# Turning the raw gate and up sums with a matrix that also adds the two halves of the rows

## The chip, the cores and the metric

The kernel runs on one core of a Trainium2 chip. The metric is the device time of one execution in microseconds (us); before the change it is 1862.35 us, the median of three runs that lie between 1861.26 and 1864.24. The profiler took one further execution of the same program, and all rows below are from that one.

## The reference, cut to what matters

The program computes two layers of a hybrid encoder trunk over 256 tokens of width 1024. The change touches only the last sublayer, a mixture of eight SwiGLU experts of which each token takes two, so that an expert sees 64 tokens on average:

```python
top_logit, top_e = lax.top_k(logits, TOP_K)          # TOP_K = 2 of N_EXPERTS = 8
def expert_block(args):                              # D_FF_EXPERT = 3584, d = 1024
    xs, e = args
    hdn = jax.nn.silu(xs @ w_gate[e]) * (xs @ w_up[e])
    return hdn @ w_down[e]
y = jnp.zeros((n, d), jnp.float32).at[row_tok].add(yb.astype(jnp.float32) * row_w[:, None])
```

All weights are float32 and are read once from memory; the eight experts hold 352 MB of them.

## The kernel before, in words

**Steps.** The 3584 hidden columns of an expert are cut into seven chunks of 512. One chunk of one expert is a step, so there are 56 steps. `expert_run` writes their order out by hand: two lanes of four experts each. Lane 0 runs its first three steps alone (`LEAD`), then steps of lane 1 and lane 0 alternate, and lane 1 ends with three steps alone. A step is: the gate sums (`gates` into the PSUM tile `ptg`), the up sums (`gates` into `ptu`), and the two halves of the down product of the step before (`down_steps`, `down`, into `ps_ye`). Each step reads six weight pieces of 128x2048 float32 (1 MiB): two of gate, two of up, two of down. `wload` loads one on the queue of SP into a buffer `wr`.

**Two ways to multiply.** How many tokens an expert got is known only on the chip, so `products` holds both ways under `tc.If(many[0])`. An expert with more than 64 tokens (here: a *full* expert) takes `passes`: each weight piece is split by ScalarE (`wh`, L327) and VectorE (`wl = wr - wh`, L333) into two float32r parts, and TensorE makes three products of 512 columns (L1415, L1418, L1419). An expert with at most 64 tokens (a *half* expert) takes `paired`: the weights are used as float32, unsplit, and two products run at once, one on each half of the array's columns (L1425). The first leaves its sum in rows 0 to 63 of the PSUM tile and the second in rows 64 to 127, each over half of the contraction.

**Adding the halves.** For a half expert the two halves of the rows have to be added. ScalarE copies the whole tile to `fe` (L1441, in `folds`), and TensorE multiplies that copy with `fold[e]`, a matrix that picks the lower half, and accumulates it into the upper half of the same PSUM tile (L1442). The fold of the gate sums is issued at the end of the half expert's branch of the up products; the fold of the up sums stands under its own `tc.If(many[2])` (L1652), between the two halves of the down product of the step before. For a full expert that block is jumped over.

**SiLU, product, turn.** Then `hs = silu(ptg) * ptu` (L1657 on ScalarE, L1661 on VectorE) is made with tokens as rows. In the next step, after its gate products, `turned` transposes it in four blocks into `ps_hT` (L1455), copies that as float32 (`hw`, L1459, used by `paired`) and splits it into `hh` and `hl` (L427, used by `passes`). The down products read `hw` or `hh` and `hl`.

**Order around it.** `in_turn` pins the order of the instructions on each engine to the order in which the code is written. `split()` issues the next weight piece, so the splits of a full expert stand among the instructions above on ScalarE and VectorE. PSUM tiles come from three pools: `qbank` with three banks (gate and up sums, gathered rows `ps_gr`), `fbank` with one (`ps_hT`, `ps_gt`, `ps_pT`), `pbank` with four (down sums). At seven places a new expert's rows are gathered (`gather`: `rows_of`, `turn_rows`, `take`, `take_whole`) while the step before it runs.

Of the kernel before, what the change touches and what calls it, by code (L numbers as in the profile page):

```python
# [20 lines left out]
P = 128  # L21
# [144 lines left out]
def tile_encoder(ctx: ExitStack, tc: tile.TileContext, a: dict, out: bass.AP, cw: dict):  # L166
# [1123 lines left out]
    def moe(l, i, xh, xl, xth, xtl):  # L1290
        with weights("r3", NX, ring=raws), tc.tile_pool(name="mo", bufs=1, reuse_waits="tile") as O:
# [58 lines left out]

            slot2 = sm("slot2")
            V.tensor_scalar(slot2, slot, -float(P), None, op0=OP.add)
# [3 lines left out]
            def gather(e, sl, lane, spare):  # L1356
# [19 lines left out]
                def rows_of(n):  # L1376
                    ns = slice(n * 512, n * 512 + 512)
                    pg = qbank("ps_gr")
                    for i, src in enumerate((xth, xtl)):
                        for hf in range(NH):  # L1380
                            keep(T.matmul(pg, pd[:, hf], src[:, hf, ns], start=i + hf == 0, stop=i + hf == NH))
                    rows = O.tile([P, 512], F32, name="rows", tag="fe", bufs=2)
                    keep(A.activation(rows, pg, AF.Copy))
                    at[n] = rows
# [17 lines left out]
            def expert_run(lanes, sl, late=False, summed=None):  # L1402
# [6 lines left out]

                def products(many, ws, h, l, hw, fold=None):  # L1410


                    def passes():
                        for j, (out, k, wh, wl, _, b, z) in enumerate(ws):
                            i = T.matmul(out, h[:, k], wh, start=b, stop=False)  # L1415
                            if j == 0:
                                turn(many, i)
                            T.matmul(out, h[:, k], wl, start=False, stop=False)  # L1418
                            T.matmul(out, l[:, k], wh, start=False, stop=z)  # L1419

                    def paired():
                        for j in range(0, len(ws), 2):
# [4 lines left out]
                        if fold:  # L1427
                            fold()

                    if many is None:  # L1430
                        passes()
                        return
                    with tc.If(many[0]) as c:
                        passes()
                    with c.Else():
                        paired()

                def folds(e, pt):

                    fe = O.tile([P, 512], F32, name="fe", tag="fe", bufs=2)  # L1440
                    in_turn(A.activation(fe, pt, AF.Copy))  # L1441
                    return lambda: T.matmul(pt[:HALF], fold[e], fe, start=False, stop=True, skip_group_check=True)  # L1442

                def gates(gs, pt, ws, many, fo):
# [6 lines left out]
                    products(many, todo, *gs, fo)  # L1451

                def turned(many, hs):
                    pT = fbank("ps_hT").rearrange("p (f t) -> p f t", f=4)
                    turn(many, *[T.transpose(pT[:, f], hs[:, f * P:f * P + P], ident) for f in range(4)])  # L1455
                    hw = None
                    if many is not None:
                        hw = O.tile([P, 4, P], F32, name="hw", bufs=1)
                        turn(many, A.activation(hw, pT, AF.Copy))  # L1459
                    hh = O.tile([P, 4, P], F32R, name="hh", tag="hh", bufs=2)  # L1460
                    hl = O.tile([P, 4, P], F32R, name="hl", tag="hl", bufs=2)
                    turn(many, *evac_split(hh, hl, pT))
                    return hh, hl, hw

                def down(many, c, cols, rows, hs, ye, ws, fo):

                    todo = []
                    for n in cols:
                        for f in rows:
# [3 lines left out]
                            todo.append((ye[n], f, dh[:, f % 2, ns], dl[:, f % 2, ns], w[:, f % 2, ns], b, z))  # L1473
                    products(many, todo, *hs, fo)

# [60 lines left out]
                def folding(e):  # L1536
                    fold[e] = O.tile([P, HALF], F32, name="fold", bufs=2)
                    V.tensor_scalar(fold[e], ident[:, HALF:], few[:, 0, e:e + 1], None, op0=OP.mult)

# [27 lines left out]

                def down_steps(many, e, c, hs, ye, by_cols=False):

                    split()  # L1570
                    parts = turned(many, hs)
                    split()
# [4 lines left out]
                    for j in range(2):  # L1577
                        cols, rows = ((j,), range(4)) if by_cols else (range(2), (2 * j, 2 * j + 1))
                        down(many, c, cols, rows, parts, ye, ws, None)
                        yield  # L1580
# [36 lines left out]
                for e in {e: 0 for e, c in steps}:  # L1617
                    n = steps.index((e, NC - 1))
                    when(n, "T", end, e)
                    when(n, "U", more, e)  # L1620
                    when(n, "S", more, e)
                    if n + 1 < len(steps):
# [10 lines left out]
                for n, (e, c) in enumerate(steps):  # L1633
                    gs, many, _, ye = states[e]
                    if c == 0 and many is not None:
# [4 lines left out]
                    gates(gs, ptg, ws[0], many, None)  # L1640
                    at(n, "G")
                    go(last)
                    at(n, "T")
                    fg = folds(e, ptg) if many is not None else None
                    gates(gs, ptu, ws[1], many, fg)
                    at(n, "U")
                    split()
                    fu = folds(e, ptu) if many is not None else None
                    at(n, "F")
                    go(last)  # L1650
                    if fu:
                        with tc.If(many[2]):  # L1652
# [11 lines left out]
                    prev = many, e, c, hs, ye  # L1664
                last, comb = down_steps(*prev, by_cols=True), states[prev[1]]
                for gen in last, last, comb, last, comb, comb:
                    go(gen)
# [114 lines left out]
```

## Time and profile before

| | |
|---|---|
| median of three runs | 1862.35 us |
| the profiled execution | 1866.12 us, of which the span from first to last instruction is 1864.3 us |
| TensorE busy over the span | 1714.2 us (92%) |
| VectorE, ScalarE, GpSimd busy | 1073.2, 907.8, 256.9 us |
| granted TensorE clock, mean | 0.953 |
| read from memory | 470.26 MB |
| the expert steps | from about 934 to 1844 us of the span |

Busy shares are means over stages with different limits. A matmul's recorded duration is longer than the distance to the next one, because they are pipelined; the cost of a matmul in a stream is therefore read from the distance of two starts. "PE" is TensorE, "PEld" its weight loads, "PEq" its sequencer, ACT ScalarE, DVE VectorE.

### The profile page before, as it was taken

The numbers are of one execution on the slowest core, as the hardware profiler recorded it, in microseconds if no ns is written. First come the engines' busy times: TensorE is split into PE (matmuls) and PEld (weight loads), VectorE is DVE, ScalarE is ACT, GpSimd is POOL, SyncE is SP. The second block draws the span as 40 slices with busy tenths as digits, with TensorE's granted clock in tenths as the row PEclk, the third lists the DMA queues.
The fourth block names the chain that finished last, engine by engine and source line by source line (L and its number), as shares of the span: only waits on it lengthen the run. The fifth ranks groups of instructions, "written<-read, shape, count | busy, mean of one in ns | idle before, by whom it ended". The sixth has DMA issues, their size and how long they took to land. (4 is left out here: it accounts for less than half of the span.)

```text
span 1864.3 us, 30071 instructions
## 1 busy us (share of the span) xinstructions
PE 1714.2 (92%) x11060; PEld 1196.4 (64%) x11060; DVE 1073.2 (58%) x1754; ACT 907.8 (49%) x1651; POOL 256.9 (14%) x248
## 2 busy tenths in 40 slices
PE   5879999899987898999889999998999999999996
PEld 5767869799977677778675554333334655655564
DVE  6888567665657986576574642210214646556476
ACT  4654445455534763345375643321214546455473
POOL 4637300000024545210100000000000000000000
PEclk8988999999998987999899999999999999999998
DMA  5331245355513332265179999999999999989992
GB/s 217 125 108 70 92 159 203 128 211 204 181 59 102 125 105 78 70 241 211 46 265 347 406 393 395 419 420 419 420 421 391 406 398 356 390 335 400 398 369 87
DMA packets 71302, 473.94 MB, mean 254 GB/s; under 512 B 8768, under 2 KB 12224, under 8 KB 15936
## 3 DMA queue, kind: packets, MB, share of 16 engines
q1 hardware_dynamic: 70384, 466.09, 64.5%
q10 hardware_dynamic: 720, 5.24, 0.8%
q8 instruction: 120, 1.97, 0.4%
q14 instruction: 78, 0.64, 0.1%
HBM read 470.26 MB, written 1.05 MB: 253 GB/s over the span
## 5 line engine op out<-in xcount | busy, mean ns | idle before, releaser
L333 DVE TENSOR_TENSOR wl<-wr,wh 128x1024 fp32r<-128x1024 f32 (+4 forms) x530 | 484.9, 965 | 141.2 <-ACT wh L327 140.3
L327 ACT ACTIVATE wh<-wr 128x1024 fp32r<-128x1024 f32 (+1 forms) x564 | 440.4, 845 | 153.6 <-PE ps_gu L1425 61.0
L1425 PE MATMUL ps_gu<-wr,gw 128*64 128x512 f32 x1120 | 266.6, 605 | 11.4 <-DMA wr<-in_moe_wg_dram 10.7
L1425 PEld LDWEIGHTS ps_gu<-wr,gw 128*64 128x64 f32 x1120 | 82.2, 138 | 160.1 <-issue 154.5
L1425 PE MATMUL ps_ye<-wr,hw 128*64 128x512 f32 x560 | 153.5, 608 | 7.4 <-PEq L1652 7.4
L1459 ACT ACTIVATE hw<-ps_hT 128x512 f32<-128x512 f32 x56 | 33.4, 597 | 234.5 <-PE ps_hT L1455 234.5
L338 POOL TENSOR_TENSOR wl<-wr,wh 128x384 fp32r<-128x384 f32 (+6 forms) x68 | 103.7, 1545 | 290.2 <-ACT wh L327 289.9
L427 DVE TENSOR_TENSOR hl<-ps_hT,hh 128x512 fp32r<-128x512 f32 x56 | 38.7, 691 | 179.1 <-ACTq L319 162.6
L1415 PE MATMUL ps_gu<-wh,xg 128*128 128x512 f32 x336 | 134.5, 400 | 2.8 <-ACT gw L1398 2.2
L1418 PE MATMUL ps_gu<-wl,xg 128*128 128x512 f32 x336 | 131.7, 392 | 0.8 <-DVE wl L333 0.8
L1419 PE MATMUL ps_gu<-wh,xg 128*128 128x512 f32 x336 | 132.1, 393 | 0.0
L1689 POOL TENSOR_TENSOR wr<-wr,lp 128x512 f32<-128x512 f32 x1 | 1.5, 1521 | 933.3 <-ACT wr L1688 933.3
L1441 ACT ACTIVATE fe<-ps_gu 128x512 f32<-128x512 f32 x112 | 66.8, 597 | 106.4 <-PE ps_gu L1419 56.0
L1661 DVE TENSOR_TENSOR hs<-hs,ps_gu 128x512 f32<-128x512 f32 x56 | 38.4, 685 | 118.3 <-PEq L1652 58.8
L1277 PE MATMUL ps_gu<-xTl,wh 128*128 128x256 f32 x352 | 99.0, 281 | 0.0
L1278 PE MATMUL ps_gu<-xTh,wl 128*128 128x256 f32 x352 | 98.8, 281 | 0.0
L1276 PE MATMUL ps_gu<-xTh,wh 128*128 128x256 f32 x352 | 98.8, 282 | 0.0
L1425 PEld LDWEIGHTS ps_ye<-wr,hw 128*64 128x64 f32 x560 | 42.2, 137 | 82.3 <-issue 78.8
L1415 PEld LDWEIGHTS ps_gu<-wh,xg 128*128 128x128 f32 x336 | 63.5, 189 | 18.6 <-ACT gw L1398 2.5
L1442 PE MATMUL ps_gu<-fe,fold 128*64 128x512 f32 x140 | 73.1, 603 | 2.4 <-ACT fe L1441 2.1
L1418 PEld LDWEIGHTS ps_gu<-wl,xg 128*128 128x128 f32 x336 | 63.6, 189 | 14.1 <-DVE wl L333 1.1
L1419 PEld LDWEIGHTS ps_gu<-wh,xg 128*128 128x128 f32 x336 | 63.5, 189 | 14.3
(466 smaller groups left out, 3723.3 us busy)
## 6 DMA issues: line engine op xcount, KB each, us to landing
wr<-in_moe_wg_dram SPq DMA_DIRECT2D x112, 1024.0 KB, 8.9
wr<-in_moe_wu_dram SPq DMA_DIRECT2D x112, 1024.0 KB, 9.2
wr<-in_moe_wd_dram SPq DMA_DIRECT2D x112, 1024.0 KB, 10.2
wr<-in_w_in_dram SPq DMA_DIRECT2D x16, 1024.0 KB, 4.9
wr<-in_ffn_wg_dram SPq DMA_DIRECT2D x11, 1024.0 KB, 4.9
wr<-in_ffn_wu_dram SPq DMA_DIRECT2D x11, 1024.0 KB, 4.9
wr<-in_ffn_wd_dram SPq DMA_DIRECT2D x11, 1024.0 KB, 4.9
wr<-in_xk_dram SPq DMA_DIRECT2D x8, 1024.0 KB, 4.8
```

The source lines that it names most:

```text
L327: act_i = A.activation(h[:, s], raw[:, s], AF.Copy)
L333: dve_i = V.tensor_sub(l[:, m], raw[:, m], R_(h[:, m]))
L338: G.tensor_sub(l[:, m], raw[:, m], R_(h[:, m]))
L1276: T.matmul(ps[:, g], wh[:, k, fs], xh[:, k, :], start=k == 0, stop=False)
L1277: T.matmul(ps[:, g], wh[:, k, fs], xl[:, k, :], start=False, stop=False)
L1278: T.matmul(ps[:, g], wl[:, k, fs], xh[:, k, :], start=False, stop=k == KT - 1)
L1415: i = T.matmul(out, h[:, k], wh, start=b, stop=False)
L1418: T.matmul(out, h[:, k], wl, start=False, stop=False)
L1419: T.matmul(out, l[:, k], wh, start=False, stop=z)
L1425: T.matmul(out[f * HALF:f * HALF + HALF], hw[:, k, :HALF], w, start=ws[j][5], stop=ws[j + 1][6], skip_group_check=True)
L1441: in_turn(A.activation(fe, pt, AF.Copy))
L1442: return lambda: T.matmul(pt[:HALF], fold[e], fe, start=False, stop=True, skip_group_check=True)
```

## The change

The raw sums of the gate and of the up product are both copied to `fe` (`taken`), for every expert. `turned` then multiplies blocks of `fe` with `fold[e]`, now 128x128: the identity and, for a half expert, a second identity that adds the lower half of the rows; for a full expert it is the identity alone. One such product turns a block and adds its halves. There are eight of them, four into `pTs[0]` (gate) and four into `pTs[1]` (up). SiLU and the product are made on the turned tiles and write `hw` directly; the copy to `hw` goes away, and so do both folds and the block under `tc.If(many[2])`. In the last step `turned` stands between the two down halves of the step before it.

```diff
-                def folds(e, pt):
-
+                def taken(pt):
                     fe = O.tile([P, 512], F32, name="fe", tag="fe", bufs=2)
-                    in_turn(A.activation(fe, pt, AF.Copy))
-                    return lambda: T.matmul(pt[:HALF], fold[e], fe, start=False, stop=True, skip_group_check=True)
+                    in_turn(A.activation(fe, pt, AF.Copy)) if sl is slot else A.activation(fe, pt, AF.Copy)
+                    return fe
...
-                def turned(many, hs):
-                    pT = fbank("ps_hT").rearrange("p (f t) -> p f t", f=4)
-                    turn(many, *[T.transpose(pT[:, f], hs[:, f * P:f * P + P], ident) for f in range(4)])
-                    hw = None
-                    if many is not None:
-                        hw = O.tile([P, 4, P], F32, name="hw", bufs=1)
-                        turn(many, A.activation(hw, pT, AF.Copy))
+                def turned(many, e, fes):
+
+                    pTs = [new("ps_hT").rearrange("p (f t) -> p f t", f=4) for new in (fbank, qbank)]
+                    for pT, fe in zip(pTs, fes):
+                        turn(many, *[T.matmul(pT[:, f], fe[:, f * P:f * P + P], fold[e], start=True, stop=True) for f in range(4)])
+                    hs = O.tile([P, 4, P], F32, name="hs", tag="hs", bufs=HSB)
+                    turn(many, A.activation(hs, pTs[0], AF.Silu))
+                    hw = O.tile([P, 4, P], F32, name="hw", bufs=1)
+                    turn(many, V.tensor_mul(hw, hs, pTs[1]))
...
-                    turn(many, *evac_split(hh, hl, pT))
+                    turn(many, *evac_split(hh, hl, hw))
...
-                    fold[e] = O.tile([P, HALF], F32, name="fold", bufs=2)
-                    V.tensor_scalar(fold[e], ident[:, HALF:], few[:, 0, e:e + 1], None, op0=OP.mult)
+                    if sl is not slot:
+                        fold[e] = ident
+                        return
+                    fold[e] = O.tile([P, P], F32, name="fold", bufs=2)
+                    lo, hi = slice(0, HALF), slice(HALF, P)
+                    V.scalar_tensor_tensor(fold[e][:, lo], ident[:, hi], few[:, 0, e:e + 1], ident[:, lo], op0=OP.mult, op1=OP.add)
+                    V.tensor_scalar(fold[e][:, hi], ident[:, hi], few[:, 1, e:e + 1], None, op0=OP.mult)
...
-                    fg = folds(e, ptg) if many is not None else None
-                    gates(gs, ptu, ws[1], many, fg)
+                    fes = [taken(ptg)]
+                    gates(gs, ptu, ws[1], many)
                     at(n, "U")
                     split()
-                    fu = folds(e, ptu) if many is not None else None
+                    fes.append(taken(ptu))
                     at(n, "F")
                     go(last)
-                    if fu:
-                        with tc.If(many[2]):
-                            in_turn(fu())
+                    prev = many, e, c, fes, ye
+                    if n == len(steps) - 1:
+                        final = down_steps(*prev, by_cols=True)
+                        go(final)
                     at(n, "D")
                     go(last)
-                    hs = O.tile([P, 512], F32, name="hs", tag="hs", bufs=HSB)
-                    turn(many, A.activation(hs, ptg, AF.Silu))
                     split()
                     at(n, "S")
                     split()
-                    turn(many, V.tensor_mul(hs, hs, ptu))
```

The same on the engines, in the order of the built program. On PE, between the gate products of a step (L1425 and before) and its up products (L1431 or L1433 and after), the four transposes stood:

```order
L1425 MATMUL ps_gu<-wr,gw_10245 64x512 x8
L1433 UNCONDITIONAL_BRANCH
L1455 MATMUL ps_hT<-consts,hs 128x128 x4
L319 UNCONDITIONAL_BRANCH x3
L1433 COMPARE_AND_BRANCH
```

and now the eight products stand there:

```order
L1425 MATMUL ps_gu<-wr,gw_10240 64x512 x8
L1431 UNCONDITIONAL_BRANCH
L1454 MATMUL ps_hT<-fold,fe 128x128 x8
L319 UNCONDITIONAL_BRANCH
L1431 COMPARE_AND_BRANCH
```

The place is the same; what is multiplied there is no longer the finished `hs`, but the two raw copies. Also on PE, between the two halves of the down product (`ps_ye`), stood the block of the second fold:

```order
L1425 MATMUL ps_ye<-wr,hw 64x512 x4
L1433 UNCONDITIONAL_BRANCH
L319 UNCONDITIONAL_BRANCH x3
L1652 COMPARE_AND_BRANCH
L1442 MATMUL ps_gu<-fe,fold 64x512
L1652 UNCONDITIONAL_BRANCH x2
L1433 COMPARE_AND_BRANCH
```

and now one half follows the other:

```order
L1425 MATMUL ps_ye<-wr,hw 64x512 x4
L1431 UNCONDITIONAL_BRANCH
L1431 COMPARE_AND_BRANCH
```

The branch L1652 is gone for all experts, the fold with it. On DVE, around the place in a step where `hl` is made, only the subtraction stood between two weight splits (L333), and the product `hs` (L1661) followed later:

```order
L333 TENSOR_TENSOR wl<-wr,wh 128x1024 x2
L319 UNCONDITIONAL_BRANCH x2
L427 TENSOR_TENSOR hl<-ps_hT,hh 128x512
L319 COMPARE_AND_BRANCH
L333 TENSOR_TENSOR wl<-wr,wh 128x1024 x2
```

and now the product stands there too:

```order
L333 TENSOR_TENSOR wl<-wr,wh 128x1024 x2
L319 UNCONDITIONAL_BRANCH x2
L1458 TENSOR_TENSOR hw<-hs,ps_hT 128x512
L427 TENSOR_TENSOR hl<-hw,hh 128x512
L319 COMPARE_AND_BRANCH
```

The product moved from the end of its own step into the chain that ends in `hw`, `hh` and `hl` of the next one. Besides, `rows` of a gather uses the buffer of `hs` in place of one of the two of `fe`, and `slot2` reuses the buffer of `sel`; a gather now meets a step in which `pTs[1]` and the up sums have the same PSUM bank.

## Rows read from the trace of the kernel before

**Rows 1.** The page: memory traffic in 40 equal slices of the span.

```profile
GB/s 217 125 108 70 92 159 203 128 211 204 181 59 102 125 105 78 70 241 211 46 265 347 406 393 395 419 420 419 420 421 391 406 398 356 390 335 400 398 369 87
```

**Rows 2.** Stretches: length, busy time by engine (x count), clock, DMA share, GB/s.

```profile
1055.38:1086.76 31.38, 30.89 (x134) 17.74 (x133) 16.75 (x17) 17.01 (x22) 0.00 (x0) 1.00 1.01 402
...
1152.15:1164.90 12.75, 12.75 (x57) 4.68 (x57) 1.38 (x2) 2.77 (x5) 0.00 (x0) 1.00 1.01 421
...
1248.82:1266.15 17.33, 14.67 (x58) 5.12 (x57) 1.38 (x2) 2.77 (x5) 0.00 (x0) 0.90 1.02 422
...
1805.55:1824.00 18.45, 18.13 (x81) 14.57 (x80) 18.19 (x20) 14.37 (x17) 0.00 (x0) 1.00 0.91 359
```

**Rows 3.** Timeline of PE over two steps: start, duration, instruction, count, [idle before].

```profile
1055.97 3.65 PE L1425 MATMUL ps_gu<-wr,gw 128*64 128x512 f32 x16
1059.65 1.07 PE L1442 MATMUL ps_gu<-fe,fold 128*64 128x512 f32 x2
1060.65 0.50 PE L1415 MATMUL ps_ye<-wh,hh 128*128 128x512 f32 x1
...
1063.64 1.07 PE L1442 MATMUL ps_gu<-fe,fold 128*64 128x512 f32 x2
...
1067.55 0.39 PE L1415 MATMUL ps_gu<-wh,xg 128*128 128x512 f32 x1
...
1073.04 0.60 PE L1455 MATMUL ps_hT<-consts,hs 128*128 128x128 f32 x4
...
1079.05 1.94 PE L1425 MATMUL ps_ye<-wr,hw 128*64 128x512 f32 x8
1081.46 1.94 PE L1425 MATMUL ps_ye<-wr,hw 128*64 128x512 f32 x8 [0.47 <-PEq L1652]
1083.23 3.60 PE L1425 MATMUL ps_gu<-wr,gw 128*64 128x512 f32 x16
1086.76 0.66 PE L1455 MATMUL ps_hT<-consts,hs 128*128 128x128 f32 x4
```

**Rows 4.** Line L1652: all that PE's sequencer did for its block.

```profile
L1652 PEldq EVENT_SEMAPHORE  x20: 51/51/51, 964.8 to 1833.6; - x20
```

**Rows 5.** Groups by line: count, busy us, mean ns, idle before.

```profile
L1442 PE MATMUL ps_gu<-fe,fold 128*64 128x512 f32 x140 | 73.1, 603 | 2.4 <-ACT fe L1441 2.1
L1455 PE MATMUL ps_hT<-consts,hs 128*128 128x128 f32 x224 | 35.4, 280 | 1.2 <-DVE hs L1661 1.2
L1459 ACT ACTIVATE hw<-ps_hT 128x512 f32<-128x512 f32 x56 | 33.4, 597 | 234.5 <-PE ps_hT L1455 234.5
L1661 DVE TENSOR_TENSOR hs<-hs,ps_gu 128x512 f32<-128x512 f32 x56 | 38.4, 685 | 118.3 <-PEq L1652 58.8 <-PE ps_gu L1442 58.2
```

**Rows 6.** Timeline of weight loads and matmuls outside the experts.

```profile
856.02 0.19 PEld L404 LDWEIGHTS ps_f<-xTl,wh 128*128 128x128 f32 x1
856.14 0.19 PEld L405 LDWEIGHTS ps_f<-xTh,wl 128*128 128x128 f32 x1
...
858.22 1.46 PE L1201 MATMUL ps_xs<-wr,qx 128*128 128x256 f32 x6
```

**Rows 7.** Timeline of PE at the start of the expert steps.

```profile
947.22 0.49 PE L1415 MATMUL ps_gu<-wh,xg 128*128 128x512 f32 x1 [0.32 <-PEq L1652]
...
951.76 0.50 PE L1418 MATMUL ps_gu<-wl,xg 128*128 128x512 f32 x1 [0.76 <-DVE wl L333]
...
955.77 0.66 PE L1455 MATMUL ps_hT<-consts,hs 128*128 128x128 f32 x4 [1.22 <-DVE hs L1661]
```

**Rows 8.** Timeline of PE at the end of the expert steps.

```profile
1838.56 0.50 PE L1415 MATMUL ps_ye<-wh,hh 128*128 128x512 f32 x1 [1.24 <-ACT hh L427]
```

**Rows 9.** Timeline of PE in a step in which rows are gathered.

```profile
1643.76 0.63 PE L1381 MATMUL ps_gr<-xtokl,pd 128*128 128x512 f32 x2
...
1649.72 0.66 PE L1389 MATMUL ps_gt<-consts,rows 128*128 128x128 f32 x4 [1.12 <-ACT gw L1398]
```

**Rows 10.** Timeline of VectorE in a full expert's step.

```profile
1068.89 2.36 DVE L333 TENSOR_TENSOR wl<-wr,wh 128x1024 fp32r<-128x1024 f32 x2
```

More of the change, by code (lines that the diff above doesn't have):

```diff
@@ L1349, in counting @@
                 V.tensor_scalar(upper, iotas, HALF - 0.5, -float(HALF), op0=OP.is_gt, op1=OP.mult)
-            slot2 = sm("slot2")
+            slot2 = sel
             V.tensor_scalar(slot2, slot, -float(P), None, op0=OP.add)
@@ L1381, in rows_of @@
                             keep(T.matmul(pg, pd[:, hf], src[:, hf, ns], start=i + hf == 0, stop=i + hf == NH))
-                    rows = O.tile([P, 512], F32, name="rows", tag="fe", bufs=2)
+                    rows = O.tile([P, 512], F32, name="rows", tag="fe" if spare is pbank else "hs", bufs=2 if spare is pbank else HSB)
                     keep(A.activation(rows, pg, AF.Copy))
@@ L1408, in expert_run, with products @@
                 turn = lambda many, *ins: [in_turn(i) for i in ins if many is not None]
-                def products(many, ws, h, l, hw, fold=None):
+                def products(many, ws, h, l, hw):
                     def passes():
@@ L1426, in paired @@
                                          skip_group_check=True)
-                        if fold:
-                            fold()
                     if many is None:
@@ L1436, in products, with gates @@
                         paired()
-                def folds(e, pt):
+                def taken(pt):
                     fe = O.tile([P, 512], F32, name="fe", tag="fe", bufs=2)
-                    in_turn(A.activation(fe, pt, AF.Copy))
-                    return lambda: T.matmul(pt[:HALF], fold[e], fe, start=False, stop=True, skip_group_check=True)
-                def gates(gs, pt, ws, many, fo):
+                    in_turn(A.activation(fe, pt, AF.Copy)) if sl is slot else A.activation(fe, pt, AF.Copy)
+                    return fe
+                def gates(gs, pt, ws, many):
                     todo = []
@@ L1450, in gates, with down @@
                             todo.append((pt, k, wh[:, k4], wl[:, k4], w[:, k4], k == 0, k == KT - 1))
-                    products(many, todo, *gs, fo)
-                def turned(many, hs):
-                    pT = fbank("ps_hT").rearrange("p (f t) -> p f t", f=4)
-                    turn(many, *[T.transpose(pT[:, f], hs[:, f * P:f * P + P], ident) for f in range(4)])
-                    hw = None
-                    if many is not None:
-                        hw = O.tile([P, 4, P], F32, name="hw", bufs=1)
-                        turn(many, A.activation(hw, pT, AF.Copy))
+                    products(many, todo, *gs)
+                def turned(many, e, fes):
[6 more added lines that the diff above has]
+                    turn(many, V.tensor_mul(hw, hs, pTs[1]))
                     hh = O.tile([P, 4, P], F32R, name="hh", tag="hh", bufs=2)
                     hl = O.tile([P, 4, P], F32R, name="hl", tag="hl", bufs=2)
-                    turn(many, *evac_split(hh, hl, pT))
+                    turn(many, *evac_split(hh, hl, hw))
                     return hh, hl, hw
-                def down(many, c, cols, rows, hs, ye, ws, fo):
+                def down(many, c, cols, rows, hs, ye, ws):
                     todo = []
@@ L1473, in down @@
                             todo.append((ye[n], f, dh[:, f % 2, ns], dl[:, f % 2, ns], w[:, f % 2, ns], b, z))
-                    products(many, todo, *hs, fo)
+                    products(many, todo, *hs)
                 def combine(e, many, ye, first):
@@ L1566, in split, with down_steps @@
                             made[key] = wload("moe_w" + w, i * NE + e, j * 4, 4, c * 512, 512, held, cond)
-                def down_steps(many, e, c, hs, ye, by_cols=False):
+                def down_steps(many, e, c, fes, ye, by_cols=False):
                     split()
-                    parts = turned(many, hs)
+                    parts = turned(many, e, fes)
                     split()
@@ L1578, in down_steps @@
                         cols, rows = ((j,), range(4)) if by_cols else (range(2), (2 * j, 2 * j + 1))
-                        down(many, c, cols, rows, parts, ye, ws, None)
+                        down(many, c, cols, rows, parts, ye, ws)
                         yield
@@ L1620, in expert_run @@
                     when(n, "U", more, e)
-                    when(n, "S", more, e)
+                    when(n, "F", more, e)
                     if n + 1 < len(steps):
@@ L1634, in expert_run @@
                     gs, many, _, ye = states[e]
-                    if c == 0 and many is not None:
+                    if c == 0:
                         folding(e)
@@ L1639, in expert_run @@
                     last = down_steps(*prev) if prev else None
-                    gates(gs, ptg, ws[0], many, None)
+                    gates(gs, ptg, ws[0], many)
                     at(n, "G")
@@ L1660, in expert_run @@
                     split()
-                    turn(many, V.tensor_mul(hs, hs, ptu))
                     at(n, "M")
                     split()
-                    prev = many, e, c, hs, ye
-                last, comb = down_steps(*prev, by_cols=True), states[prev[1]]
-                for gen in last, last, comb, last, comb, comb:
+                last, comb = final, states[prev[1]]
+                for gen in last, comb, last, comb, comb:
                     go(gen)
```

## The prediction

> **What bounds the kernel now.** Only the expert steps change, so I read these alone, first by memory traffic. In the slices of the page from the 21st on [rows 1] traffic is 390 to 420 GB/s; in a block of six slices it stands at 419 to 421, elsewhere a little lower. The stretches say why [rows 2]. Where both lanes hold half experts, traffic is 421 GB/s with a DMA share of 1.01. A step there brings six pieces of 1 MiB (6.29 MB), which is 14.9 us at that rate, while TensorE needs 12.75 us when it still has pieces in hand and stretches to 17.33 us when it waits. That block, some 270 us long, is bound by memory: what TensorE saves in it is worth nothing. Where a half and a full expert alternate, a pair of steps takes 31.38 us at 402 GB/s and TensorE is busy for 30.89 of them; memory alone would need 2 x 14.9 = 29.9 us. That stretch is bound by TensorE, with only 1.5 us per pair between the two bounds. Where full experts run alone (three steps at each end) a step takes 18.45 us, TensorE is busy for 18.13 and VectorE for 18.19.
>
> The number of steps of each kind follows from the code and from one row: 140 records of the fold [rows 5] are 35 steps with two folds of two records (a float32 product is made in two passes, each a record). So 35 of 56 steps belong to half experts and 21 to full ones, three experts. The order of the products on PE shows which: the first of lane 0 and the last two of lane 1. Of their 21 steps 3 run alone at the start and 3 at the end; 4 and 11 alternate with half steps. So there are 15 pairs that TensorE bounds, and 6 lone full steps. The sum goes over these alone.
>
> **The turn.** Four transposes become eight float32 products of 128 columns, 16 passes in place of 4. Four transposes take 0.60 us with the last one's tail; a single one has a mean of 0.28 [rows 5], so they follow each other at (0.60 - 0.28) / 3 = 0.107 us [rows 3]. No float32 product with 128 weight columns and 128 moving columns stands in the trace. Bounds: from below the transpose's 0.107. Six passes of 256 columns take 1.46 us, less a tail of 0.38 that is 0.216 each [rows 6]: two cycles per column, so 128 columns stream in 0.108 too. What could be slower is the weight load. Loads of 128x128 follow each other at 0.12 us where the products are short [rows 6], and each one lasts 0.19. From above I take that 0.19. The nearest row is the stream of loads, and I use 0.115, between it and the transposes. The turn then costs 16 x 0.115 - 4 x 0.107 = +1.41 us per step. A page's rule on the load stands here for comparison. The Trainium skill (TensorE: Matmul & The Clock Gate, LDWEIGHTS) prices a weight load by its columns over 1.2 GHz, 107 ns for 128; by it the turn would cost 16 x 0.107 - 0.43 = +1.28 us, and the trace's 0.12 us is a little worse.
>
> **The folds (half steps).** The two folds take 1060.65 - 1059.65 = 1.00 us each [rows 3]. Ahead of the first PE waits for the copy: the up products take 3.68 us where the same sixteen passes take 3.53 in the gate products, 0.15. The half of the down product between the folds takes 1063.64 - 1060.65 = 2.99 us, where twelve passes in one run take 5.49 / 2 = 2.75; with no switch between the halves I give back 0.2 for both. Together -2.35 us. With the turn a half step changes by -0.94.
>
> **The skipped block (full steps).** For a full expert the block L1652 is jumped over, and that is not free. Eight passes that start at 1079.05 should hand over after 8 x 0.215 = 1.72 us, at 1080.77; the next start is at 1081.46 [rows 3], 0.69 us later, and PE's sequencer is named. The block leaves a semaphore event on 20 of the 21 full steps [rows 4]. With down products of a full expert the loss is smaller, near 0.47 us (0.32 idle [rows 7] and a slow first pass, estimated at 0.15). Without the block two such halves follow each other with about 0.05. So -0.64 with the turn +1.41 is +0.77 us for a full step in a pair, and -0.45 + 1.41 = +0.96 for a lone one.
>
> **Pairs.** -0.94 + 0.77 = -0.17, for 15 pairs -2.6 us. A pair of 31.2 us stays above memory's 29.9, so memory does not cut it off.
>
> **Start.** In the first two steps SiLU and the product stand ahead of the splits of the next weights, and the turn waits for them: idle times of 0.32, 0.76 and 1.22 us [rows 7], 2.3 in all, and with the slow passes behind them (0.3 each, estimated) some 3.2 us. After the change both come later and the splits are made sooner; TensorE needs the copies alone. VectorE has little in hand there, so I count 2.4 of the 3.2. Two turns +2.8, one skip -0.45: together -0.1 us.
>
> **End.** Two turns of lone full steps +2.8; two skips -0.9. The last turn now takes 1.84 us, its own 0.60 and 1.24 of waiting for the copies, which nothing covers [rows 8]; after the change it stands ahead of a down half of 2.75 us, which covers the chain, and costs 1.84 + 0.1. Together +2.0 us.
>
> **Gathers.** Four of the seven gathers lie in stretches that TensorE bounds. There the second transposition of rows waits for the chain of evictions on ScalarE, not for PE: 5.3 us from the end of `ps_gr` to `ps_gt` [rows 9], with a fold lying in that wait. So the fold's 1.0 us, or the skip's 0.6, is not gained there. Besides the up sums have the bank of `pTs[1]` and must wait for VectorE's product; `ps_gr` covers most of it. I take +1.0 for two half steps and +0.6 for two full ones, +3.2 us.
>
> **What costs nothing.** ScalarE loses a copy of 0.60 us per step, and VectorE keeps its count [rows 5]; in the pairs they are busy for 17 of 31.4 us [rows 2]. The chain from the turn to `hh` grows from two copies to SiLU, product and copy, 0.6 + 0.69 + 0.6 = 1.9 us. The up products, 3.5 us at least, lie over it. VectorE's product stands right behind a weight split of two pieces, 2.36 us, which before is done 1.8 us ahead of the turn (1071.25 against 1073.04) [rows 10, 3]. If that cover went, the down product would wait; that is a rival below. The new matrix is two small instructions per expert on VectorE, ahead of its steps. No DMA is added or moved.
>
> **Sum.** -2.6 - 0.1 + 2.0 + 3.2 = +2.5 us. The profiled execution's 1866.12 us would become 1868.6; it lay 3.8 us above the median of the runs, so against 1862.35 I get about 1864.9. I count the uncertain terms (0.2 for the switch between halves, 0.8 kept back at the start) half towards the gain and forecast **1864 us**, no change that a measurement can tell: for this kernel 0.2%, 3.7 us, is about what can be told from none. Its own range is 1859 to 1868.
>
> **Rivals.**
> (a) *Faster.* The pitch is 0.107, the wait at the start goes entirely, and the gathers keep their gain: the turn then costs 1.28, 0.13 less at each of the 34 turns in TensorE-bound steps (-4.4), the start -0.8, the gathers -3.2. That is -5.9 us against the sum, about **1857**. For it: transposes do run at 0.107, and PE is nowhere idle for ScalarE once folds are gone. Against: 0.12 in the stream of loads, and the wait at `ps_gt` is not PE's.
> (b) *Slower by the weight loads.* If a load of float32 weights is not hidden behind a stream as short as itself, the pitch goes towards 0.19: 34 x 16 x 0.075 = +41 us at the end of that, 1905; halfway, at 0.145, +16 us and **1880**. It decides from 0.12 on, where it adds 2.7 us. Against: loads already follow each other at 0.12 with a product under way.
> (c) *Slower by the chain.* If VectorE's product comes a whole weight split later (2.36 us), the chain lasts 4.5 us against 3.5 of cover in the 15 half steps of the pairs: +15 us, **1879**. It decides once the product is more than 1.4 us late. Against: VectorE is busy for half of that stretch, and before the change it waits for the turn rather than the turn for it.
> (d) *The skip is worth less.* If the stall at L1652 is the drain between two products of different kind, which stays, only the branch instruction itself is saved. From rows the gain would then be only the idle time that names the sequencer's wait event, 0.05 us [rows 4], in place of 0.64 and 0.45: 15 x 0.59 + 3 x 0.4 = +10 us, **1874**. Against: 0.47 us of the gap are put down to the sequencer. The rule of a page would be close to it: the Trainium skill (Advanced Engine Details and Errata, Control Flow Timing) gives 108 ns for a compare-and-branch and 51 ns for a branch, by which the skip would be worth 0.16 us, the time about 1872. The rows do not bear it out, since the gap is four times that.
>
> **Chances.** Forecast 0.45, (a) 0.25, (b) 0.13, (c) 0.09, (d) 0.08. So faster by over 0.2% 0.25, within 0.2% 0.45, slower 0.30. The range that leaves out the far half of (b) and the tails of (a) and (c) is 1854 to 1879.
>
> **What would show it.** In the profile after: 16 passes of the turn at 0.11 to 0.12 us from start to start, about 1.9 us between gate and up products; pairs of about 31.2 us; no gap between two down halves of a full step (now 0.69); the first turn some 2 us earlier than at 955.77; the half-expert block unchanged at about 420 GB/s; two lone full steps at the end about 1 us longer each; a wait of about 1 us more ahead of `ps_gt` in a gather. The prediction is wrong if the turn's pitch is above 0.13, if the down products wait for `hh` or `hw`, or if a pair falls to memory's 29.9 us.

## The result, and the profile after

The changed kernel takes 1887.38 us (median of four runs, 1884.91 to 1889.74) against 1862.15: a ratio of 1.0134, with an interval of 1.0114 to 1.0154. That is 25 us slower. The forecast was 1864 and its range 1854 to 1879, so the prediction was wrong. The profiled execution has a span of 1887.8 us, 23.5 more than before.

First the work itself. The timeline of PE in the changed kernel, over a half and a full step, answers to [rows 3]:

```profile
1054.00 2.05 PE L1454 MATMUL ps_hT<-fold,fe 128*128 128x128 f32 x16
1055.98 3.65 PE L1425 MATMUL ps_gu<-wr,gw 128*64 128x512 f32 x16
1059.57 0.50 PE L1415 MATMUL ps_ye<-wh,hh 128*128 128x512 f32 x1
...
1070.88 1.95 PE L1454 MATMUL ps_hT<-fold,fe 128*128 128x128 f32 x16
...
1078.22 3.65 PE L1425 MATMUL ps_ye<-wr,hw 128*64 128x512 f32 x16
1081.71 3.60 PE L1425 MATMUL ps_gu<-wr,gw 128*64 128x512 f32 x16
```

The turn takes 1.98 us in the half step (1055.98 - 1054.00), and in the full step that follows the sixteen passes of the down product (the half expert's, from the step before) run through in 3.49 us with no gap (1081.71 - 1078.22). The windows of the changed kernel for such a pair, a step of the memory-bound block and a lone full step answer to [rows 2] (length, busy time by engine, clock, DMA share, GB/s):

```profile
1054.00:1085.24 31.24, 31.24 (x154) 20.38 (x153) 16.74 (x17) 16.12 (x20) 0.00 (x0) 1.00 0.99 406
1155.18:1167.61 12.43, 12.43 (x66) 5.22 (x64) 1.38 (x2) 2.42 (x4) 0.00 (x0) 1.00 1.01 422
1825.67:1844.92 19.25, 19.25 (x94) 16.06 (x93) 18.27 (x19) 13.80 (x16) 0.00 (x0) 1.00 0.88 339
```

A pair is 31.24 us where it was 31.38. So the ordinary steps do what was forecast, and the loss must lie in steps that are not ordinary. Setting the start of every turn on PE against the same turn of before gives the place (each length is the distance of two starts in the two timelines; the sums of four and two steps are added up):

| stretch of the expert steps | before, us | after, us | difference | forecast |
|---|---|---|---|---|
| start, up to the second turn | 43.21 | 39.50 | -3.71 | -1.4 |
| ordinary pairs | 408.81 | 406.80 | -2.01 | -2.4 |
| four gathering steps in TensorE-bound stretches | 80.57 | 100.60 | **+20.03** | +4.4 |
| two steps in which a half expert ends ahead of a full step | 37.75 | 41.79 | **+4.04** | with the pairs |
| memory-bound block | 288.11 | 288.99 | +0.88 | 0 |
| end, the last four turns and the products behind them | 55.86 | 59.97 | **+4.11** | +2.0 |

With the 0.24 us by which the stage begins later they make 23.6 us, the 23.5 of the span to the rounding. The forecast column puts each term of the prediction where its steps lie: of the two turns counted in the start (+1.41 each) the second falls in the first gathering step. The four gathering steps are most of the loss. The worst of them is 26.04 us long in place of 18.62. PE in that step of the changed kernel:

```profile
1560.21 1.95 PE L1454 MATMUL ps_hT<-fold,fe 128*128 128x128 f32 x16
1565.16 1.22 PE L1381 MATMUL ps_gr<-xtokh,pd 128*128 128x512 f32 x2 [3.01 <-DVE pd L1361]
...
1567.46 0.63 PE L1418 MATMUL ps_gu<-wl,xg 128*128 128x512 f32 x1
1567.89 0.63 PE L1419 MATMUL ps_gu<-wh,xg 128*128 128x512 f32 x1
```

PE waits 3.01 us for `pd`, the one-hot matrix that picks the rows to be gathered. Then nine passes follow each other at 0.43 us in place of 0.23. Why `pd` is late stands in the timeline of VectorE at the same place:

```profile
1553.29 2.36 DVE L333 TENSOR_TENSOR wl<-wr,wh 128x1024 fp32r<-128x1024 f32 x2 [1.47 <-ACT wh L327]
1562.19 0.28 DVE L1541 SCALAR_TENSOR_TENSOR fold<-consts,few 128x64 f32<-128x64 f32 x1 [6.55 <-PE ps_hT L1454]
1562.40 0.25 DVE L1542 TENSOR_SCALAR fold<-consts,few 128x64 f32<-128x64 f32 x1
1562.56 2.35 DVE L333 TENSOR_TENSOR wl<-wr,wh 128x1024 fp32r<-128x1024 f32 x2
1564.83 0.48 DVE L1361 TENSOR_SCALAR pd<-consts,slot 128x128 fp32r<-128x128 f32 x2
1565.45 0.69 DVE L1458 TENSOR_TENSOR hw<-hs,ps_hT 128x512 f32<-128x512 f32 x1
```

VectorE stands for 6.55 us before the small instruction that makes the fold matrix of the *next* expert, and waits for PE's turn (L1454). The matrix has two buffers. The turn that runs here is the last one that reads the matrix of the lane's old expert, and the new matrix goes into that buffer. Behind the blocked instruction stand a pair of weight splits, then `pd`, then the product. In the code the matrix is made one step later than `pd`; since `in_turn` does not pin it, the built order could put it ahead of `pd` on VectorE, as it did before the change too. The view of waits (total, times, longest) of the changed kernel shows that the blocked instruction stands at every gather but the first:

```profile
DVE fold L1541 <- PE ps_hT L1454: 64.2, 6, 12.0
```

The same instruction waited in the kernel before as well, 25.3 us in five places (L1442 are the folds, the readers of that time), and PE had no wait for `pd` in the expert steps:

```profile
DVE fold L1538 <- PE ps_gu L1442: 14.9, 3, 5.1
...
DVE fold L1538 <- PEq L1652: 10.4, 2, 5.2
```

In two other gathering steps the same blocked queue shows twice, ahead of the gathered rows and ahead of the up sums. The PE timeline of one:

```profile
1120.13 0.73 PE L1381 MATMUL ps_gr<-xtokh,pd 128*128 128x512 f32 x2 [0.98 <-DVE pd L1361]
1123.39 5.35 PE L1425 MATMUL ps_gu<-wr,gw 128*64 128x512 f32 x16 [2.06 <-DVE hw L1458]
```

The second wait is for the product, because the up sums of this step have the PSUM bank of the turned up sums. The last two places: where a half expert ends, and the last step.

```profile
1546.89 0.58 PE L1488 MATMUL ps_pT<-gate,pg 128*128 128x1 f32 x4 [1.94 <-DVE pg L1484]
...
1862.13 0.50 PE L1415 MATMUL ps_ye<-wh,hh 128*128 128x512 f32 x1 [1.51 <-ACT hh L427]
```

### The profile page after: what moved, and what is told of

Its sections match the earlier page's. It is cut to its first block, busy times and chain, and to the rows that moved or that the text cites. A ratio compares the mean times of both kernels' runs of the same rounds, so it can differ in the third digit from the quotient of the medians.

```text
span 1887.8 us, 30968 instructions
## 1 busy us (share of the span) xinstructions
PE 1726.9 (91%) x11592; PEld 1258.0 (67%) x11592; DVE 1076.0 (57%) x1762; ACT 887.2 (47%) x1595; POOL 257.0 (14%) x248
## 5 line engine op out<-in xcount | busy, mean ns | idle before, releaser
L333 DVE TENSOR_TENSOR wl<-wr,wh 128x1024 fp32r<-128x1024 f32 (+4 forms) x530 | 483.9, 965 | 183.4 <-ACT wh L327 182.5
L1425 PE MATMUL ps_gu<-wr,gw 128*64 128x512 f32 x1120 | 259.8, 603 | 13.2 <-DMA wr<-in_moe_wg_dram 9.0
L1425 PEld LDWEIGHTS ps_gu<-wr,gw 128*64 128x64 f32 x1120 | 78.4, 138 | 164.2 <-issue 145.6
L1458 DVE TENSOR_TENSOR hw<-hs,ps_hT 128x512 f32<-128x512 f32 x56 | 38.5, 687 | 196.8 <-PE ps_hT L1454 190.7
L1456 ACT ACTIVATE hs<-ps_hT 128x512 f32<-128x512 f32 x56 | 33.4, 597 | 243.4 <-PE ps_hT L1454 243.4
L1425 PE MATMUL ps_ye<-wr,hw 128*64 128x512 f32 x560 | 131.4, 606 | 2.7 <-DMA wr<-in_moe_wd_dram 2.3
L1454 PEld LDWEIGHTS ps_hT<-fold,fe 128*128 128x128 f32 x896 | 106.2, 191 | 27.3 <-issue 13.8
L1454 PE MATMUL ps_hT<-fold,fe 128*128 128x128 f32 x896 | 112.3, 278 | 0.0
L1425 PEld LDWEIGHTS ps_ye<-wr,hw 128*64 128x64 f32 x560 | 37.3, 137 | 78.5 <-issue 64.0
```

Source lines behind the costliest of these rows:

```text
L333: dve_i = V.tensor_sub(l[:, m], raw[:, m], R_(h[:, m]))
L1454: turn(many, *[T.matmul(pT[:, f], fe[:, f * P:f * P + P], fold[e], start=True, stop=True) for f in range(4)])
```

## The experiments

The first four were made against the changed kernel, each undoing one suspect. All times stand beside the kernel before on the same chip.

**e1: make the fold matrix later.**

```diff
-                    if c == 0:
-                        folding(e)
                     ptg, ptu = qbank("ps_gu"), qbank("ps_gu")
...
+                    if c == 0:
+                        folding(e)
                     at(n, "D")
```

and the two instructions in `folding` are wrapped in `in_turn`.

> The changed kernel (1887.4 us) with the two instructions that make the fold matrix of a new expert moved on VectorE from the start of the expert's first step to its second half, and pinned there. Theory 1 (VectorE is blocked: the new matrix needs the buffer that the turn of the expert before still reads, so the one-hot matrix of the gathered rows, a pair of weight splits and the product queue up behind it): the waits of 3.01, 0.98 and 0.98 us ahead of the gathered rows and two of the three waits for the product's PSUM bank (2.06 each) go, with the slow passes after the longest: 8 to 12 us, about 1877. Theory 2 (the gathers lose their time only because the turned up sums and the next up sums share a bank): PE waits in the same places for the product instead, under 2 us, about 1886.

Measured: 1869.99 us against 1861.10, 1.0045 (1.0028 to 1.0061). That is 17.4 us less than the changed kernel's median (16.6 by the two ratios), more than theory 1 expected, which counted slow passes behind one wait only. In the changed kernel the up products behind the two waits of 2.06 us are slow too (5.35 us in place of 3.65, at a granted clock of 0.68 and 0.67). The three gathering steps fall by 4.9, 5.8 and 3.9 us; the first gather, which no fold matrix blocks, stays at 21.6. VectorE and PE in the worst step of before, now with this edit:

```profile
1552.47 0.48 DVE L1361 TENSOR_SCALAR pd<-consts,slot 128x128 fp32r<-128x128 f32 x2
1556.37 0.69 DVE L1458 TENSOR_TENSOR hw<-hs,ps_hT 128x512 f32<-128x512 f32 x1 [3.42 <-PE ps_hT L1454]
```

```profile
1554.31 1.95 PE L1454 MATMUL ps_hT<-fold,fe 128*128 128x128 f32 x16
1556.02 0.71 PE L1381 MATMUL ps_gr<-xtokh,pd 128*128 128x512 f32 x2
```

`pd` is ready 1.4 us before the turn begins, the rows follow the turn without a wait, and the up sums of these steps no longer wait for the product either, although the banks are as they were. Theory 1 holds. The edit both moves and pins the two instructions; which of the two is needed was not separated.

**e2: another bank for the first gathered rows.**

```diff
-                    pg = qbank("ps_gr")
+                    pg = (fbank if spare is fbank and n == 0 else qbank)("ps_gr")
```

> The changed kernel with the first gathered rows put into the bank of the turned gate sums, so that the up sums of a gathering step get a bank of their own. Theory 1 (VectorE's blocked queue is the larger part): the waits of 1.32, 2.06 and 2.06 us for the product go, but the rows now wait some 0.6 us for SiLU and the later rows for the same late chain: 2 to 4 us, about 1884. Theory 2 (the shared bank is the whole loss of the gathers): 10 us or more, about 1876.

Measured: 1881.17 us, 1.0104 (1.0084 to 1.0124), 6.2 less than the changed kernel. That lies between the two theories. The first gather falls by 1.4 us, two others by 2.4 each. The wait for `pd` stays in all three steps that have a blocked matrix, 1.07 us in two and 3.10 us in the third. One of them:

```profile
1116.48 0.70 PE L1381 MATMUL ps_gr<-xtokh,pd 128*128 128x512 f32 x2 [1.07 <-DVE pd L1361]
```

The shared bank is a part of the loss; only in the first gather is it all that goes beyond the turn itself (+1.45 us is left there, for a turn of +1.35). With the fold matrix out of the way (e5 against e1, by step) the bank is worth 1.5 us in the first gather, 0.1 in two others and 1.1 in the last.

**e3: a free buffer for the last product.**

```diff
-                    hw = O.tile([P, 4, P], F32, name="hw", bufs=1)
+                    hw = O.tile([P, 4, P], F32, name="hw", tag="fe" if final else "hw", bufs=2 if final else 1)
```

> The changed kernel with the last step's product written into a free buffer (one of fe) and not into the single buffer hw, which the second down half of the step before still reads. If the wait is for that buffer, the product follows SiLU by itself and PE's wait of 1.51 us ahead of the last down products goes: 1.5 to 2 us less, about 1885.6, and SiLU to product falls from 3.1 us to about 0.1. If the chain itself is too long for the cover of one down half, the wait stays above 1 us.

Measured: 1885.05 us, 1.0124 (1.0104 to 1.0145); the last step falls by 2.0 us. VectorE and then ScalarE at the end of the changed kernel, and VectorE of e3:

```profile
1860.73 0.69 DVE L1458 TENSOR_TENSOR hw<-hs,ps_hT 128x512 f32<-128x512 f32 x1 [3.67 <-PE ps_ye L1419]
...
1857.03 0.60 ACT L1456 ACTIVATE hs<-ps_hT 128x512 f32<-128x512 f32 x1 [1.41 <-PE ps_hT L1454]
```

```profile
1855.05 0.69 DVE L1458 TENSOR_TENSOR hw<-hs,ps_hT 128x512 f32<-128x512 f32 x1 [0.87 <-PE ps_hT L1454]
```

In the changed kernel the product waits for PE's down products (`ps_ye`), 3.1 us beyond the end of SiLU: `hw` has one buffer, and the down half that was meant to cover the chain may itself read it. In e3 it starts 0.3 us after SiLU's end at 1854.75, and PE has no wait there.

**e4: the compares of an ended expert ahead of the product.**

```diff
-                    when(n, "T", end, e)
+                    when(n, "G", end, e)
```

> The changed kernel with the compares of a finished expert's weights (pg) issued on VectorE ahead of the turn's product, and not behind it. If the two waits of 1.94 us ahead of ps_pT come from the longer chain (SiLU, product) that now stands ahead of these compares, both go: 3 to 4 us less, about 1884. If they come from the weight splits ahead of them, they stay and the time stays within 1 us of 1887.4.

Measured: 1879.70 us, 1.0089 (1.0066 to 1.0113), 7.7 less. Both waits are gone; the compares `pg` now come 14 us ahead of their reader:

```profile
1529.46 0.48 DVE L1484 TENSOR_SCALAR pg<-cols,slot 128x128 f32<-128x128 f32 x2
...
1543.56 0.61 PE L1488 MATMUL ps_pT<-gate,pg 128*128 128x1 f32 x4
```

The two steps fall from 20.9 to 17.35 us, 3.5 each and not the 1.94 of the wait, and to 1.5 below the kernel before. The rest is the clock, below.

**e5: all four edits.**

> The changed kernel with all four edits of the first runs: fold matrix made later, first gathered rows in the other bank, the last product in a free buffer, pg ahead of the product. By the steps in which each of them gained (17.4 for the first, 1.4 that the second adds in the first gather, 2.0 for the third, 5.5 that the fourth adds to the first): about 1861, as before the change. If the edits stand in each other's way (pg and the gathers share VectorE), 1866 or more.

Measured: 1860.57 us, 0.9997 (0.9986 to 1.0009). The edits add up; the time is that of the kernel before, to between -2.6 and +1.7 us. So the four account for the loss of the changed kernel. What is left of the change is worth nothing that can be told; the prediction's sum of +2.5 us lies a little above that interval. By stretch e5 keeps gains and losses of its own: against the kernel before the gathers stand at +2.7 us and the end at +1.8, the start at -2.8, the ordinary pairs at -2.0 and the two steps of e4 at -3.0.

**e6: transposes in place of products,** on top of e5. The halves are not added here, and no fold matrix is made.

```diff
-                        turn(many, *[T.matmul(pT[:, f], fe[:, f * P:f * P + P], fold[e], start=True, stop=True) for f in range(4)])
+                        turn(many, *[T.transpose(pT[:, f], fe[:, f * P:f * P + P], ident) for f in range(4)])
```

> As e5, with eight plain transposes in place of the eight float32 products of the turn. It leaves out the adding of the halves of half experts, so it only measures what the products cost. Theory 1 (a product costs two passes of 0.106 us, a transpose one): a turn is 0.85 us shorter; in the pairs of half and full steps the cycle falls from 31.24 to some 29.6 to 29.9 us, where memory binds, and the time falls by 20 to 28 us against e5, to about 1837. Theory 2 (the turn's price is its start and the switch to full width, not the passes): under 8 us.

Measured: 1830.70 us, 0.9850 (0.9833 to 0.9868), 29.9 below e5, a little more than theory 1 gave. The group of the turn and the window of one pair:

```profile
L1454 PE MATMUL ps_hT<-consts,fe 128*128 128x128 f32 x448 | 59.8, 276 | 0.0
```

```profile
1050.40:1079.70 29.30, 29.30 (x138) 18.39 (x137) 16.77 (x17) 16.15 (x21) 0.00 (x0) 1.00 1.01 420
```

448 records against 896 in the changed kernel: one pass for a transpose, two for a product. TensorE is busy for the whole 29.3 us and memory is at the 420 GB/s of the block: both bounds meet here.

**e7: the halves added behind the transposes.**

```diff
+                    up = O.tile([P, 4, HALF], F32, name="up", bufs=1)
+                    for pT, to in zip(pTs, (hs[:, :, :HALF], up)):
+                        turn(many, A.activation(to, pT[:, :, HALF:], AF.Copy, scale=few[:, 0, e:e + 1]))
+                    for pT, to in zip(pTs, (hs[:, :, :HALF], up)):
+                        turn(many, V.tensor_add(pT[:, :, :HALF], pT[:, :, :HALF], to))
                     turn(many, A.activation(hs, pTs[0], AF.Silu))
```

> As e6, with the halves added behind the turn: ScalarE copies the upper 64 columns of both turned tiles, scaled by 1 for a half expert and 0 for a full one, and VectorE adds them to the lower 64 columns, before SiLU. Four instructions of 256 columns more in the chain, some 1.6 us. If the up products (3.5 us and more) still cover the chain, the time is that of e6 within 3 us and beats both kernels; if not, PE waits for hw or hh in each of the 30 steps of the pairs, up to 1 us each, and it ends near 1855.

Measured: 1848.18 us, 0.9939 (0.9916 to 0.9961). It beats both kernels and leaves nothing out, but 17.5 us of e6 are lost. In most pairs the time is that of e6 (15.78 and 13.50 us for the two halves of a pair in both); by step, 7.0 us stand in the first two steps, 4.6 in the last two, and most of the rest at gathers and just behind them. In a lone full step VectorE had no room before either [rows 2]. PE of e7 in three such places:

```profile
960.19 0.50 PE L1415 MATMUL ps_ye<-wh,hh 128*128 128x512 f32 x1 [1.18 <-ACT hh L427]
976.46 1.22 PE L1381 MATMUL ps_gr<-xtokh,pd 128*128 128x512 f32 x2 [3.77 <-ACT hs L1462]
...
1668.46 0.49 PE L1415 MATMUL ps_ye<-wh,hh 128*128 128x512 f32 x1 [0.98 <-ACT hh L427]
```

**e8: the kernel before, with SiLU behind the splits.**

```diff
-                    turn(many, A.activation(hs, ptg, AF.Silu))
                     split()
                     at(n, "S")
                     split()
+                    turn(many, A.activation(hs, ptg, AF.Silu))
                     turn(many, V.tensor_mul(hs, hs, ptu))
```

> The kernel before the change with nothing but SiLU moved behind the two weight splits that follow it (the product is already there). If what the change gained at the start (4.2 us up to the first turn) is SiLU and its table load standing ahead of the splits on ScalarE, the first turn comes 3 to 4 us earlier than 955.77 and the time is 2 to 4 us lower, about 1858.5. If it is the product on VectorE, which stays where it is, under 1 us.

Measured: 1860.61 us, 0.9999 (0.9989 to 1.0009): no difference that can be told. The stretch from the first gate product to the first turn, in this kernel and then in the changed one:

```profile
928.78 0.78 PE L1415 MATMUL ps_gu<-wh,xg 128*128 128x512 f32 x1 [2.24 <-ACT gw L1398]
...
948.61 0.66 PE L1455 MATMUL ps_hT<-consts,hs 128*128 128x128 f32 x4 [1.12 <-DVE hs L1661]
```

```profile
933.36 0.79 PE L1415 MATMUL ps_gu<-wh,xg 128*128 128x512 f32 x1 [2.24 <-issue]
951.57 1.95 PE L1454 MATMUL ps_hT<-fold,fe 128*128 128x128 f32 x16
```

It is 19.83 us here, 18.21 in the changed kernel and 21.72 before (934.05 to 955.77). So SiLU ahead of the splits accounts for 1.9 of the 3.5 us, and the product, for which PE still waits 1.12 us ahead of the turn, for most of the rest. The gain shows in the trace and is too small for the times.

**e9 and e10: the chain ahead of the splits.** e9 is e7 with the split behind the turn; e10 is e9 without the edit of e2.

```diff
-                    split()
                     parts = turned(many, e, fes, by_cols)
+                    split()
                     split()
```

> As e7 (1848.2 us), with the weight split that stood ahead of the turn's SiLU, adds and product on ScalarE and VectorE issued behind them. If what e7 loses against e6 is that the chain stands behind a pair of weight splits (waits of 1.18, 3.77, 0.98 and about 1.3 us twice, and some 4 us in the last two steps), most of it goes: 4 to 8 us, about 1842. If the weights then come too late, PE waits for wl or wh in the steps of full experts and the time is that of e7 or above.

> As e9, with the first gathered rows back in the bank of before (the second edit of e5 undone). In e7 these rows wait for SiLU, which is now longer in coming, in three gathers (3.77, 1.29, 1.28 us). If the bank matters with the longer chain, these waits become waits of the up sums for the product, as in the changed kernel: the same time within 2 us. If the rows gain by their own bank and the up sums have cover, 3 us or more less than e9.

Measured: 1859.18 us, 0.9987 (0.9974 to 1.0000), and 1858.60 us, 0.9972 (0.9961 to 0.9984). Both lose against e7, 9 and 6 us by the ratios (11 and 10 by the medians). That is the second case of the expectation of e9: the weights come too late. The bank makes no difference that can be told, as the first theory of e10 had it. The first gather gains (25.6 to 20.8 us) and so do the last two steps (2.9 us together), but each pair now waits for a split and is some 1.6 us longer than in e7. PE of e9:

```profile
1027.45 0.50 PE L1418 MATMUL ps_ye<-wl,hh 128*128 128x512 f32 x1 [0.76 <-DVE wl L333]
1028.59 0.50 PE L1418 MATMUL ps_ye<-wl,hh 128*128 128x512 f32 x1 [0.17 <-DVE wl L333]
```

In a pair the split serves ahead of the chain, in the first gather and at the end behind it; one fixed place serves only one of them.

## Why the prediction was wrong

**The step that failed** is the sentence under "What costs nothing": "The new matrix is two small instructions per expert on VectorE, ahead of its steps." They are small, 0.28 and 0.25 us, but they have to wait for the last reader of a buffer, and that reader had moved. Before, the matrix was read by the folds of its own step. Now the turn of the *next* step reads it. I priced the duration and did not ask whom the instruction waits for and what is queued behind it. The old instruction already waited 25.3 us in the kernel before, but PE waited for no `pd`. The change put its release behind PE's turn, and the gathered rows, which need `pd`, come right behind that turn. e1 takes the two instructions to another place and 17.4 us go.

**Gathers.** The four steps were forecast at +4.4 us, 3.2 of it for what is lost in them, and rose by 20.0. The shared bank was seen ("must wait for VectorE's product; `ps_gr` covers most of it"), but the product was taken to come in time. It came behind the blocked matrix. With the four edits (e5) the rise is 2.7 us.

**pg.** Rival (c), the later chain, was looked for at the down products, where the cover held: PE waits for `hh` or `hw` in no ordinary pair. It came true at another reader. `pg` stands behind the chain on VectorE, and the two steps where a half expert ends became 2.0 us longer each (e4).

**End.** The size was off, +4.1 for +2.0. The term assumed that the down half of 2.75 us covers the chain; the product could not start until that half was done, since `hw` has one buffer (e3: 2.0 us).

**Start.** The forecast kept back too much: -3.7 us where -1.4 was counted up to the second turn. The waits ahead of the first turn went whole.

**Turn, folds, skip.** These steps held. The turn rose by 1.39 us in a half step (1.98 - 0.59) and 1.35 in a full one (1.70 - 0.35) for a forecast of 1.41: sixteen passes at 0.106 us, so rival (b) is out. The Trainium skill (TensorE: Matmul & The Clock Gate, LDWEIGHTS) prices a weight load at its columns divided by 1.2, in ns, an estimate of 107 ns for 128, and the pitch here agrees with it. It does not show that the load sets the pitch: the stream of 128 columns, read from the rows before at 0.108 us, takes as long. Up products, two folds and the down product of a half step fell from 11.57 to 9.29 us, by 2.28 for 2.35. The two halves of the down product in a full step fell from 4.18 to 3.49 us, 0.69 for 0.64, so rival (d) is out too. The Trainium skill (Advanced Engine Details and Errata, Control Flow Timing) gives the times of the two branches, by which the block is 0.16 us, an estimate; the measurement decides, and the skipped block between these products cost 0.69 us. Together a pair went down by 0.14 us for a forecast of 0.17.

**Memory.** That the half-expert block gives nothing back held: 288.1 and 289.0 us. Its steps come faster by 0.3 us while pieces are in hand (12.75 to 12.43) and then wait longer.

**Slips in the sums.** The sum counts no step for two places that TensorE bounds: the gathering step between the first four pairs and the memory-bound block (by its own terms -0.94), and one of the three lone steps ahead of the last turn (+0.96). That the two cancel is luck. The -5.9 us of rival (a) is against the kernel before; against the sum its terms make -8.4. The chain of rival (c) adds up to 4.3 us (1.9 + 2.36) and not 4.5, so its price is 11 us and not 15; halfway in rival (b) is 0.153 us and not 0.145. In [rows 1] the slices at 419 to 421 GB/s are five, not six, and those from the 21st on lie between 265 and 421 (without the last), not all at 390 and above. None of these bears on the cause.

Rival (a) was nearest to right on the engines' rows (pitch 0.106, the whole wait at the start) and wrong in the time, since none of the rivals had VectorE blocked.

## What to carry to other kernels

When a read of a buffer moves to a later step, price the *next write* of that buffer: find where its instruction stands on its engine and name what is queued behind it, however small it is. Covers hold for the ordinary step and fail at the seams (a gather, the end of an expert, the last step); count those apart, with each buffer that the moved chain now holds. And a turn by plain transposes had half the passes of one by float32 products here, so adding the halves elsewhere was worth 12 us here, as long as the engine that adds has room.

## What the runs showed of the hardware that was not expected

A wait of PE can cost more than its length. After the wait of 3.01 us the granted clock of the changed kernel fell to half (1.2 of 2.4 GHz). Windows of the changed kernel, the seventh number being the clock:

```profile
1565.16:1571.20 6.04, 6.04 (x14) 4.78 (x15) 1.53 (x3) 1.72 (x3) 0.00 (x0) 0.50 0.16 68
1571.30:1574.50 3.20, 3.20 (x15) 2.57 (x14) 0.00 (x0) 0.00 (x0) 0.00 (x0) 1.00 0.00 0
```

The gathered rows and up sums of that step took 2.9 us more than at the full clock (1.88 for 1.00, 7.46 for 5.49), which nearly doubles the wait. It does not fall each time. Behind the wait of 1.94 us for `pg` the clock was 0.78 over the next down products in the changed kernel, and 1.00 in e1 behind a wait of the same length (the windows stand in this order):

```profile
1547.60:1554.70 7.10, 7.10 (x26) 5.69 (x25) 5.39 (x6) 4.35 (x6) 0.00 (x0) 0.78 0.96 389
```

```profile
1543.00:1550.00 7.00, 7.00 (x33) 5.71 (x33) 6.60 (x6) 5.49 (x8) 0.00 (x0) 1.00 1.02 425
```

The step was 1.6 us shorter in e1 by that alone, which is also why single steps of an experiment can move by as much without any edit near them.
